# Moving the left tiles by 32 bytes, norm_mix out of the turned blocks, and two pages exchanged, in a hybrid encoder layer

## The chip, the cores and the metric

The kernel runs on one core of one Trainium2 chip. The metric is the device time of one execution in microseconds; lower is better. A core has TensorE (PE; its weight loads are listed apart as PEld), VectorE (DVE), ScalarE (ACT), GpSimd (POOL) and SyncE (SP), which issues most DMAs. Each engine works through its own queue in order.

## The reference, cut to what matters

One layer of an encoder trunk, in float32, on x of 2048 tokens by 1024 features:

```python
h = rms_norm(x, norm_mix[l])
z = h @ w_in[l]
q_a, k_a, v_a, q_b, k_b, v_b, g_a, g_b = jnp.split(z, offsets, axis=-1)
y_a = windowed_gqa(...)       # 8 heads, |t - s| <= 128
y_b = neighborhood_attn(...)  # 8 heads on the 32 x 64 grid of tokens
merged = gates[..., :D] * (y_a @ w_proj_a[l]) + gates[..., D:] * (y_b @ w_proj_b[l])
x = x + merged @ w_out[l]
h2 = rms_norm(x, norm_mlp[l])
x = x + jnp.square(jax.nn.relu(h2 @ w_up[l])) @ w_down[l]
return rms_norm(x, norm_final)
```

rms_norm divides a token's row by its root mean square and multiplies by a gain for each feature.

## The kernel before

**Arithmetic.** Every float32 product is made of three matmuls on float32r parts. An operand t is split into hi (a cast on ACT) and lo (t - hi, on DVE or POOL: `split`, L281), and a product is hi.hi + hi.lo + lo.hi (`mm3`, L199; `mm3s`, L285). In a call `mm3(ps, lh, ll, rh, rl)` the l operands are the weights that TensorE holds (128 x 128) and the r operands are read past them (128 x 512). In a row of the profile such as `zb<-zh,zwhl` zh is read and zwhl is held. The large products for the first 1024 tokens of the input projection, for the up and the down projection are done in two by two blocks with seven block products in place of eight (Strassen's form); the loops over them go through the numbers 1 to 7 in the order 1, 2, 5, 6, 7, 4, 3 (`ORDER`, L352) or another, and each number has its page of right operands, a hi and a lo tile of 128 x 2048 elements: `zh1` to `zh7` in the input projection, `ubh1` to `ubh7` (rows `ubh`) in the up projection.

**Stages, in order of time.** The microseconds are from the span's start, read off the rows.
- 0 to some 380 us: input projection of token blocks 0 and 1 (512 tokens each). x's rows are loaded, normalised, turned by TensorE (`turned`, L274) and multiplied by norm_mix as they leave PSUM (L497 to L501). Nine groups of columns (`QUADS`, L503) are then computed by `in_quad` (L457). Before the last page sums are made, t1 = hi + lo of page 1 is formed on POOL (L537 to L539), placed behind two of the roots that `rstd_of` (L220) computes on POOL.
- Within it, at quads 5 and 6 (L626 to L632), the rows of token blocks 2 and 3 are loaded (`x_tiles`, L343), normalised by DVE (`normalised`, L233) and turned by DVE in blocks of 32 x 32 (`turned_out`, L241), multiplied by norm_mix there (L254, with `gt` from `turned_gain`, L259) and stored to DRAM as h1d.
- 380 to some 1080 us: `h_pages` (L651) loads h1d and splits it into the pages hT, and TensorE alternates between the dense products of blocks 2 and 3 (`mm<-hT,whl`, L200 to L202) and the two attentions.
- 1080 to some 1455 us: gates and output projections (`gated`, L1279), the product with w_out (`pt<-wo,mh`), the residual, and the second norm; `turned_out` writes the turned rows h2d, again with a gain (norm_mlp). For the last of the four token blocks it works in the tile mh (L1339).
- some 1455 to 2080 us: up projection, `up_quad` (L1198), with its pages made by `up_right` (L1131). 2080 us to the end: down projection (L1388 to L1525).

**A turned block's tokens.** Tile t of a block has 128 tokens. A turn in 32 x 32 blocks puts token 128 t + 32 a + c of the block into column 128 a + 32 t + c. Whoever reads h1d or h2d restores the order with `by_place` and `by_token` (L266 to L272).

**Memory.** Each partition of on-chip memory is filled from both ends. Left tiles go upward from 0: 1024 bytes of DMA scratch, four constants at 32 bytes, then the pool cp with ident (512 bytes), g_mix (32), bg (64), sink_t (32), warm and four st tiles (each padded to 32). That makes 1952 bytes, which is 416 modulo 512, and since the tiles behind are whole multiples of 512, all of them lie at 416: zh1, zh2, zh6, zh7, zh4, hT, wo, mh, ml, xr, and the left tiles of the attentions. Right tiles go downward; `power` takes the uppermost 64 bytes, and the others lie at 448 modulo 512: zh5, zh3, zwhl, whl, page, and everything of the up and down projections, whose lowest tile, ubh4, starts at 1984.

Space is used again: a tile that lies where an older one lay waits until that one's last reader is done. In the up projection the homes are given out downward in the order of `up_homes` (L1348), into the place of the output projection's left tiles. Those are, upward: wo to 67488, five xr buffers to 87968, gt to 90016, mh to 106400 and ml to 122784. Page 6 lies at 106432 to 122816, page 2 at 90048 to 106432, and page 3 at 73664 to 90048.

**Order.** The framework orders the instructions of each engine by a simulated timeline when the program is compiled, so they don't run strictly in the order of the source; `tc.issue_after(i)` puts what it encloses behind i on the same engine.

Of the kernel before, what the change touches and what calls it, by code (L numbers as in the profile page):

```python
# [8 lines left out]
F32 = mybir.dt.float32  # L9
F32R = mybir.dt.float32r  # L10
AF = mybir.ActivationFunctionType
ALU = mybir.AluOpType
# [3 lines left out]
D = 1024  # L16
# [6 lines left out]
P = 128  # L23
KC = D // P
NB = 4
BT = 512
# [66 lines left out]
def encoder_layer(ctx, tc, x, norm_mix, w_in, b_gate, sink, rpb, w_pa, w_pb, w_out,  # L93
                  norm_mlp, w_up, w_down, norm_final, dist_a, mask_b, out):
    nc = tc.nc
    V, A, G, PE, SY = nc.vector, nc.scalar, nc.gpsimd, nc.tensor, nc.sync
# [9 lines left out]
    def pools(stack, side, tags, name):  # L106

        return {t: pool(f"{name}_{t}", side=side, stack=stack) for t in tags}

    cp = pool("cp", side="left")  # L110
# [13 lines left out]
    def T(pl, shape, dt, tag, bufs):  # L124
        n_t[0] += 1
        pl = pl[tag] if isinstance(pl, dict) else pl
        return pl.tile(shape, dt, tag=tag, bufs=bufs, name=f"{tag}_{n_t[0]}")
# [2 lines left out]
    ident = cp.tile([P, P], F32, name="ident")  # L130
    make_identity(nc, ident)
    g_mix = cp.tile([P, KC], F32, name="g_mix")
    bg = cp.tile([P, 16], F32, name="bg")
    sink_t = cp.tile([P, AH], F32, name="sink_t")
    power = cr.tile([P, 1], F32, name="power")
    G.memset(power, -0.5)
# [20 lines left out]
    h1d = [dp.tile([D, BT], F32, name=f"h1d{b}") for b in range(2)]  # L157
# [53 lines left out]
    last_dma = [None]  # L211
# [3 lines left out]
        last_dma[0] = SY.dma_start(t, rows).ins  # L215
        return t

    roots = []

    def rstd_of(pl, t, jp=None, mean=False):  # L220

        st = T(pl, [P, 4], F32, "st", 4)
        junk = T(pl if jp is None else jp, [P, 512], F32, "junk", 1)
        for n in range(2):
            A.activation(junk, t[:, n * 512 : (n + 1) * 512], AF.Square, scale=float(D) ** -0.5 if mean else 1.0,
                         accum_out=st[:, n : n + 1])
        r = st[:, 2 : 3]
        V.scalar_tensor_tensor(out=r, in0=st[:, 0:1], scalar=EPS if mean else D * EPS, in1=st[:, 1:2],
                               op0=ALU.add, op1=ALU.add)
        roots.append(G.tensor_tensor(out=r, in0=r, in1=power, op=ALU.pow).ins)  # L230
        return r

    def normalised(pl, tiles, jp=None, by_scalar=False):  # L233

        for t in tiles:
            if by_scalar:
                A.activation(t, t, AF.Copy, scale=rstd_of(pl, t, jp, True))
            else:
                V.tensor_scalar(t, t, rstd_of(pl, t, jp), float(D) ** 0.5, ALU.mult, ALU.mult)

    def turned_out(d, ht, tiles, g, gain=None, queue=None):  # L241

        hv = ht.rearrange("p (j t c) -> p t j c", j=8, t=4)
        for t in range(4):
            V.transpose(out=hv[:, t], in_=tiles[t][:, g * 256 : (g + 1) * 256].rearrange("p (j c) -> p j c", j=8))
        h3 = ht.rearrange("p (j x) -> p j x", j=8)  # L250
        if gain is not None:
            (step, n), _ = gain.ap
            gv = bass.AP(gain.tensor, gain.offset + 8 * g, [[step, n], [1, 8], [0, P]])
            V.tensor_tensor(out=h3, in0=h3, in1=gv, op=ALU.mult)  # L254
        dv = d.rearrange("(j i) (a x) -> a i j x", i=32, a=4)
        for a in range(4):
            (queue or SY).dma_start(dv[a][:, 8 * g : 8 * g + 8], h3[32 * a : 32 * a + 32])

    def turned_gain(t, norm):  # L259

        for a in range(4):
            SY.dma_start(t[32 * a : 32 * a + 32, 32:64], norm[0].rearrange("(j i) -> j i", i=32))
        V.transpose(out=t[:, 0:32], in_=t[:, 32:64])
        return t[:, 0:32]

    def by_token(c):  # L266

        return c.rearrange("p (t a c) -> p t a c", t=4, a=4)

    def by_place(c):  # L270

        return c.rearrange("p (a t c) -> p t a c", t=4, a=4)  # L272
# [5 lines left out]
    def add(eng, out, a, b, op=ALU.add):  # L278
        return eng.tensor_tensor(out=out, in0=a, in1=b, op=op).ins  # L279

    def split(src, hi, lo, eng):  # L281
        A.copy(hi, src)  # L282
        return eng.tensor_tensor(out=lo, in0=src, in1=hi.bitcast(F32), op=ALU.subtract).ins  # L283
# [6 lines left out]
    def halves(t):  # L290

        return t[:, 0:2], t[:, 2:4]
# [13 lines left out]
    xf = x[0]  # L306
    s_z = ExitStack()
# [14 lines left out]
    xp = pools(s_x, "left", ("xin",), "x0")  # L322
# [4 lines left out]
    in_e = ring(s_z, "ze", [P, 2, BT], F32, 2)  # L327
# [15 lines left out]
    def x_tiles(pl, b, bufs):  # L343
        out = []
        for t in range(4):
            xt = T(pl, [P, D], F32, "xin", bufs) if t < bufs else in_v2[0]()
            r = b * BT + t * P
            last_dma[0] = SY.dma_start(xt, xf[r : r + P]).ins
            out.append(xt)
        return out  # L350

# [5 lines left out]

    def left_parts(src, w, eng):
        hl = in_whl()[:, :, :, 0:w]
        split(src, hl[:, 0], hl[:, 1], eng)  # L360
        return hl

    def in_left(ws, w, skip=()):

# [151 lines left out]
    tiles[1] = x_tiles(xp, 1, 8)  # L516
    ws1.append(row_half(*QUADS[1], 1))
    with tc.issue_after(last_dma[0]), nc.allow_non_contiguous_dma(reason="small per-feature vectors"):
        SY.dma_start(bg, b_gate[0].rearrange("(k p) -> p k", p=P))
        SY.dma_start(sink_t, bcast(sink[0], AH))  # L520
    normalised(xp, tiles[0])
    right = {n: (in_page[n](), in_page[n]()) for n in (1, 2)}
    tbanks = [(tpool, 2), (zpool[0], 1), (tpool, 2), (zpool[1], 1), (ypool[0], 1), (ypool[1], 1)]
    for k in range(KC):
        ps = zbank(*tbanks[k % 6])
        turned(ps, tiles[0], k)
        h, l = (t[:, k % 4] for t in right[1 + k // 4])
        scaled(h, ps, k)
        scaled_less(l, ps, k, h.bitcast(F32))
    t1, t3 = in_raw(), in_raw()  # L530
# [3 lines left out]
    next(quad0)  # L534
    next(quad0)
    normalised(xp, tiles[1], by_scalar=True)
    for n, (o, h, l) in enumerate(zip(halves(t1), *map(halves, right[1]))):  # L537
        with tc.issue_after(roots[6 + n]):
            add(G, o, h.bitcast(F32), l.bitcast(F32))  # L539
    next(quad1)  # L540
    next(quad1)

# [7 lines left out]
    for p in range(2):  # L550
        t = T(xp, [P, D], F32, "xin", 8).rearrange("p (k c) -> p k c", k=4)
        c = QUADS[2][0]
        SY.dma_start(t, w_in[0][p * BT : (p + 1) * BT, c : c + 256].rearrange("(k p) f -> p k f", p=P))
        ops2.append(left_parts(t, 256, V))
        next(quad2)
    for n in (5, 3, 6):
        right[n] = (in_page[n](), in_page[n]())
# [5 lines left out]
    for k in range(KC):  # L563
# [8 lines left out]
        else:  # L572
            h, l = (t[:, kk] for t in right[3])
# [41 lines left out]
    for q in range(2, len(QUADS)):  # L615
        if q == 5:
            s_v.close()
            in_v2.pop()
            xp = pools(s_z, "right", ("xin", "st", "gt"), "x2")
            gain = turned_gain(T(xp, [P, 64], F32, "gt", 1), norm_mix)  # L620
        if q == 7:
            bias_tables()
        lf = list(in_left(ws, 256, (1, 2) if q == 2 else ()))
        if q + 1 < len(QUADS):
            ws = in_weights(*QUADS[q + 1])
        if q in (5, 6):  # L626

            b = q - 3
            xt = x_tiles(xp, b, 3)
            normalised(xp, xt, Junk())  # L630
            for g in range(4):
                turned_out(h1d[b - 2], in_e().rearrange("p k x -> p (k x)"), xt, g, gain)  # L632
        ops2.extend(lf if q == 2 else ())
        for _ in quad2 if q == 2 else in_quad(*QUADS[q], iter(lf), right):
            pass
# [15 lines left out]
    def h_pages(b):  # L651
        hi, lo = [], []
        for p in range(2):
            h, l = (T(hpl[2 * (b - 2) + p], PAGE, F32R, "hT", 2) for _ in range(2))
            for n, (hh, ll) in enumerate(zip(halves(h), halves(l))):
                raw = T(wp, [P, KC, P], F32, "raw", 3).rearrange("p (k a) c -> p k (a c)", k=2)
                r = p * BT + n * 256
                SY.dma_start(raw, h1d[b - 2][r : r + 256, :].rearrange("(k p) t -> p k t", p=P))
                for k in range(2):
                    split(by_place(raw[:, k]), by_token(hh[:, k]), by_token(ll[:, k]), V)  # L660
            hi.append(h)
            lo.append(l)
        hp[b] = hi, lo
# [339 lines left out]
    h2d = [dp.tile([D, BT], F32, name=f"h2d{b}") for b in range(NB)]  # L1003
    s_wo = ExitStack()
    pwo = pool("pwo", side="left", stack=s_wo)
    p4x = pools(s_wo, "left", ("xr", "gt", "mh", "ml"), "m")

    p4x["st"] = cp
    gain = turned_gain(T(p4x, [P, BT], F32, "gt", 1)[:, 0:64], norm_mlp)
# [36 lines left out]
    def up_homes(*tags):  # L1046
        made = {}
        for t in tags:
            shape, dt, bufs = {"raw": (PAGE, F32, 5), "whla": ([P, 2, 4, 256], F32R, 1), "whlb": ([P, 2, 4, 256], F32R, 2),
                               "S": ([P, 4, 256], F32, 2), "rb": (PAGE, F32, 1), "chunk": ([P, BT], F32, 4),  # L1050
                               "c": ([P, BT], F32, 11)}.get(t, (PAGE, F32R, 2))
            made[t] = ring(s_up, f"u{t}", shape, dt, bufs)
            if t[:2] == "bh":
                up_page[int(t[2])] = made[t]
        up_rings.update(made)
# [289 lines left out]

    s_pp.close()
    pms.extend(pool(f"pm{i}", space=PSUM) for i in range(8))
    up_homes("bh6", "bh2", "bh3", "chunk", "rb", "c", "bh7", "bh4")  # L1348
    rights, lf = started
    for m in range(2):  # L1350
        right = next(rights)
# [204 lines left out]
```

## Time and profile before

| | |
|---|---|
| time, median of 3 runs | 2700.07 us (2696.72 to 2704.57) |
| the profiled execution | 2699.71 us, span 2697.3 us |
| busy: PE, PEld, DVE, ACT, POOL | 2620.9, 2159.8, 1600.8, 1230.6, 850.4 us |
| mean granted TensorE clock | 0.992 |
| PE busy from 230 to 300 us (input projection, blocks 2 and 3 normalised) | 64.41 of 70.00 us |
| PE busy from 1440 to 1500 us (start of the up projection) | 50.16 of 60.00 us |
| PE busy from 1500 to 2080 us, and from 2080 to 2697 us | 569.69 of 580.00 us, 608.75 of 617.00 us |

The span runs from the first to the last instruction; the execution's time has a little more around it. A row of the groups gives line, engine, operation, tiles, shapes and count, then busy time and mean ns of one, then the engine's idle time just before and what ended it. A row in order of time gives start, duration, the same names, and in brackets the idle time before it. Matmuls overlap in the pipeline, so their durations are longer than the distance from one start to the next; the distance is what a matmul costs.

### The profile page before, as it was taken

The numbers are of one execution on the slowest core, as the hardware profiler recorded it, in microseconds if no ns is written. First come the engines' busy times: TensorE is split into PE (matmuls) and PEld (weight loads), VectorE is DVE, ScalarE is ACT, GpSimd is POOL, SyncE is SP. The second block draws the span as 40 slices with busy tenths as digits, with TensorE's granted clock in tenths as the row PEclk, the third lists the DMA queues.
The fourth block names the chain that finished last, engine by engine and source line by source line (L and its number), as shares of the span: only waits on it lengthen the run. The fifth ranks groups of instructions, "written<-read, shape, count | busy, mean of one in ns | idle before, by whom it ended". The sixth has DMA issues, their size and how long they took to land. (4 is left out here: it accounts for less than half of the span.)

```text
span 2697.3 us, 34681 instructions
## 1 busy us (share of the span) xinstructions
PE 2620.9 (97%) x12140; PEld 2159.8 (80%) x12140; DVE 1600.8 (59%) x2418; ACT 1230.6 (46%) x2257; POOL 850.4 (32%) x671
## 2 busy tenths in 40 slices
PE   7999999999999999999998999999999999999998
PEld 6787777787888888787786888878887888888887
DVE  7766656666444443655657666775565634545766
ACT  6333236666555555623323544454444332323444
POOL 1111223334555542532430455664553000000001
PEclk9999999999999999999999999999999999999999
DMA  5656375446776664854644665764436834445555
GB/s 176 192 155 195 118 236 148 116 113 177 210 223 191 184 180 142 300 157 145 202 144 143 229 224 202 251 232 153 163 113 226 314 140 170 145 149 171 179 192 168
DMA packets 352751, 490.31 MB, mean 182 GB/s; under 512 B 27561, under 2 KB 187433, under 8 KB 350401
## 3 DMA queue, kind: packets, MB, share of 16 engines
q1 hardware_dynamic: 345664, 471.31, 55.1%
q10 hardware_dynamic: 6912, 16.78, 1.7%
q8 instruction: 96, 1.57, 0.2%
q14 instruction: 79, 0.64, 0.1%
HBM read 328.55 MB, written 159.45 MB: 181 GB/s over the span
## 5 line engine op out<-in xcount | busy, mean ns | idle before, releaser
L287 PE MATMUL b<-dwh,dah 128*128 128x512 f32 x896 | 348.9, 389 | 0.0
L288 PE MATMUL b<-dwh,dah 128*128 128x512 f32 x896 | 348.0, 389 | 0.0
L286 PE MATMUL b<-dwh,dah 128*128 128x512 f32 x896 | 339.3, 391 | 2.0 <-ACT dwh L282 2.0
L279 POOL TENSOR_TENSOR uc<-uc,uc 128x512 f32<-128x512 f32 x120 | 235.8, 1980 | 196.8 <-ACT uc L1196 161.5
L282 ACT CAST dah<-da 128x1024 fp32r<-128x1024 f32 (+1 forms) x128 | 121.0, 945 | 366.2 <-PE b L288 242.7
L283 DVE TENSOR_TENSOR dah<-da,dah 128x1024 fp32r<-128x1024 f32 (+1 forms) x128 | 139.2, 1089 | 221.2 <-ACT dah L282 217.2
L286 PE MATMUL b<-ubh,uwhlb 128*128 128x512 f32 x592 | 230.6, 390 | 4.4 <-DVE uc L279 1.7
L288 PE MATMUL b<-ubh,uwhlb 128*128 128x512 f32 x592 | 229.6, 389 | 1.1 <-DVE uwhlb L283 1.1
L287 PE MATMUL b<-ubh,uwhlb 128*128 128x512 f32 x592 | 230.3, 389 | 0.0
L200 PE MATMUL mm<-hT,whl 128*128 128x512 f32 x544 | 220.2, 405 | 0.0
L201 PE MATMUL mm<-hT,whl 128*128 128x512 f32 x544 | 216.5, 398 | 0.0
L202 PE MATMUL mm<-hT,whl 128*128 128x512 f32 x544 | 216.3, 398 | 0.0
L177 POOL TENSOR_TENSOR whl<-raw,whl 128x1024 fp32r<-128x1024 f32 x66 | 165.6, 2510 | 158.8 <-ACT whl L176 140.4
L1446 POOL TENSOR_TENSOR st<-st,power 128x1 f32<-128x1 f32 x16 | 13.5, 857 | 615.8 <-DVE st L1445 615.8
L286 PE MATMUL zb<-zh,zwhl 128*128 128x512 f32 x476 | 190.8, 402 | 12.1 <-DVE zc L279 6.3
L286 PEld LDWEIGHTS b<-dwh,dah 128*128 128x128 f32 x896 | 168.7, 188 | 37.5 <-ACT dwh L282 2.4
L287 PEld LDWEIGHTS b<-dwh,dah 128*128 128x128 f32 x896 | 168.5, 188 | 35.1
L288 PEld LDWEIGHTS b<-dwh,dah 128*128 128x128 f32 x896 | 168.4, 188 | 35.0
L279 DVE TENSOR_TENSOR uc<-b,uc 128x512 f32<-128x512 f32 x160 | 108.4, 687 | 143.0 <-PE b L288 128.5
L287 PE MATMUL zb<-zh,zwhl 128*128 128x512 f32 x476 | 190.0, 399 | 0.0
L288 PE MATMUL zb<-zh,zwhl 128*128 128x512 f32 x476 | 187.3, 399 | 1.8 <-DVE zwhl L283 1.8
L286 PEld LDWEIGHTS b<-ubh,uwhlb 128*128 128x128 f32 x592 | 111.1, 188 | 28.9 <-issue 2.4
(250 smaller groups left out, 6192.0 us busy)
## 6 DMA issues: line engine op xcount, KB each, us to landing
at<-uc SPq DMA_DIRECT2D x224, 256.0 KB
da<-at SPq DMA_DIRECT2D x96, 512.0 KB
dw<-in_w_down_dram SPq DMA_DIRECT2D x160, 256.0 KB
uraw<-in_w_up_dram SPq DMA_DIRECT2D x32, 1024.0 KB
raw<-in_w_in_dram SPq DMA_DIRECT2D x34, 512.0 KB
zraw<-in_w_in_dram SPq DMA_DIRECT2D x16, 1024.0 KB
z<-zg SPq DMA_DIRECT2D x64, 256.0 KB
qa<-qs_a SPq DMA_DIRECT2D x32, 256.0 KB
```

What stands on the lines that cost most here:

```text
L177: G.tensor_tensor(out=hl[:, 1], in0=raw, in1=hl[:, 0].bitcast(F32), op=ALU.subtract)
L200: PE.matmul(ps, lh, rh, start=first, stop=False)
L201: PE.matmul(ps, lh, rl, start=False, stop=False)
L202: PE.matmul(ps, ll, rh, start=False, stop=last)
L279: return eng.tensor_tensor(out=out, in0=a, in1=b, op=op).ins
L282: A.copy(hi, src)
L283: return eng.tensor_tensor(out=lo, in0=src, in1=hi.bitcast(F32), op=ALU.subtract).ins
L286: PE.matmul(ps, lh, rh, start=first, stop=False, skip_group_check=True)
L287: PE.matmul(ps, lh, rl, start=False, stop=False, skip_group_check=True)
L288: PE.matmul(ps, ll, rh, start=False, stop=last, skip_group_check=True)
L1446: G.tensor_tensor(out=r, in0=r, in1=power, op=ALU.pow)
```

## The change

Six edits. bg is allocated with 24 columns in place of 16, of which 16 are used; the left tiles behind it lie 32 bytes higher, at 448 modulo 512. For token blocks 2 and 3, x's rows are loaded so that tile t holds tokens 128 a + 32 t + c, and the turned columns then stand in the tokens' own order. norm_mix is no longer multiplied into the turned blocks; `h_pages` applies it while it splits, as the scale of ACT's copy and in DVE's subtraction. The normalisation of these two blocks goes from DVE (`tensor_scalar`) to ACT (an activation with a scale). The two adds that make t1 go from POOL to DVE, behind the lo part of the first extra operand of quad 2. And two pairs of homes change places: gt and xr on the left side, and the up projection's pages 2 and 3.

```diff
-    bg = cp.tile([P, 16], F32, name="bg")
+    bg = cp.tile([P, 24], F32, name="bg")
...
-        roots.append(G.tensor_tensor(out=r, in0=r, in1=power, op=ALU.pow).ins)
+        G.tensor_tensor(out=r, in0=r, in1=power, op=ALU.pow)
...
             r = b * BT + t * P
-            last_dma[0] = SY.dma_start(xt, xf[r : r + P]).ins
+            rows = xf[r : r + P]
+            if b > 1:
+
+                rows = bass.AP(xf.tensor, xf.offset + (b * BT + t * 32) * D, [[P * D, 4], [D, 32], [1, D]])
+            last_dma[0] = SY.dma_start(xt, rows).ins
...
-        split(src, hl[:, 0], hl[:, 1], eng)
+        last_part[0] = split(src, hl[:, 0], hl[:, 1], eng)
...
-        SY.dma_start(bg, b_gate[0].rearrange("(k p) -> p k", p=P))
+        SY.dma_start(bg[:, 0:16], b_gate[0].rearrange("(k p) -> p k", p=P))
...
-    for n, (o, h, l) in enumerate(zip(halves(t1), *map(halves, right[1]))):
-        with tc.issue_after(roots[6 + n]):
-            add(G, o, h.bitcast(F32), l.bitcast(F32))
...
         ops2.append(left_parts(t, 256, V))
+        if p == 0:
+            with tc.issue_after(last_part[0]):
+                for o, h, l in zip(halves(t1), *map(halves, right[1])):
+                    add(V, o, h.bitcast(F32), l.bitcast(F32))
...
-            xp = pools(s_z, "right", ("xin", "st", "gt"), "x2")
-            gain = turned_gain(T(xp, [P, 64], F32, "gt", 1), norm_mix)
+            xp = pools(s_z, "right", ("xin", "st"), "x2")
...
-            normalised(xp, xt, Junk())
+            normalised(xp, xt, Junk(), by_scalar=True)
             for g in range(4):
-                turned_out(h1d[b - 2], in_e().rearrange("p k x -> p (k x)"), xt, g, gain)
+                turned_out(h1d[b - 2], in_e().rearrange("p k x -> p (k x)"), xt, g)
...
                 for k in range(2):
-                    split(by_place(raw[:, k]), by_token(hh[:, k]), by_token(ll[:, k]), V)
+                    gain = g_mix[:, p * 4 + n * 2 + k : p * 4 + n * 2 + k + 1]
+                    A.activation(hh[:, k], raw[:, k], AF.Copy, scale=gain)
+                    V.scalar_tensor_tensor(out=ll[:, k], in0=raw[:, k], scalar=gain, in1=hh[:, k].bitcast(F32),
+                                           op0=ALU.mult, op1=ALU.subtract)
...
-    p4x = pools(s_wo, "left", ("xr", "gt", "mh", "ml"), "m")
+    p4x = pools(s_wo, "left", ("gt", "xr", "mh", "ml"), "m")
...
-    up_homes("bh6", "bh2", "bh3", "chunk", "rb", "c", "bh7", "bh4")
+    up_homes("bh6", "bh3", "bh2", "chunk", "rb", "c", "bh7", "bh4")
```

More of the change, by code (lines that the diff above doesn't have):

```diff
@@ L216, in load_tile @@
         return t
-    roots = []
     def rstd_of(pl, t, jp=None, mean=False):
@@ L359, in left_parts @@
         hl = in_whl()[:, :, :, 0:w]
-        split(src, hl[:, 0], hl[:, 1], eng)
+        last_part[0] = split(src, hl[:, 0], hl[:, 1], eng)
         return hl
+    last_part = [None]
     def in_left(ws, w, skip=()):
```

## The prediction

> **What bounds the kernel now.** I read the page's busy table first, then the groups of instructions, then TensorE's rows in order of time, then its waits.
>
> ```profile
> PE 2620.9 (97%) x12140; PEld 2159.8 (80%) x12140; DVE 1600.8 (59%) x2418; ACT 1230.6 (46%) x2257; POOL 850.4 (32%) x671
> ...
> L287 PE MATMUL b<-dwh,dah 128*128 128x512 f32 x896 | 348.9, 389 | 0.0
> ...
> L201 PE MATMUL mm<-hT,whl 128*128 128x512 f32 x544 | 216.5, 398 | 0.0
> ...
> L287 PE MATMUL zb<-zh,zwhl 128*128 128x512 f32 x476 | 190.0, 399 | 0.0
> ...
> L201 PE MATMUL pt<-wo,mh 128*128 128x512 f32 x256 | 99.9, 392 | 0.0
> ```
>
> TensorE is busy for 97% of the span and no other engine for more than 59%. So time goes only in two ways: a matmul that takes longer than it must, or a gap on TensorE. The four groups have one shape. In the first and the last both operands lie on one side of the memory (dwh and dah right, wo and mh left): 389 and 392 ns. In the two between, which read left pages against right weights (zb's right pages among them), it is 398 and 399 ns. Left tiles start at 416 modulo 512 bytes, right ones at 448.
>
> Means hold stalls, so I compare bare runs. In the fourth quad products 3 and 4 take turns, twelve matmuls each; 3 reads the right page zh3, 4 the left page zh4, both against zwhl on the right. The last two rows are from the down projection, 24 matmuls apart.
>
> ```profile
> 161.36 0.39 PE L286 MATMUL zb<-zh,zwhl 128*128 128x512 f32 x1
> ...
> 164.11 0.40 PE L286 MATMUL zb<-zh,zwhl 128*128 128x512 f32 x1
> ...
> 166.91 0.39 PE L286 MATMUL zb<-zh,zwhl 128*128 128x512 f32 x1
> ...
> 169.65 0.40 PE L286 MATMUL zb<-zh,zwhl 128*128 128x512 f32 x1
> ...
> 2299.63 0.39 PE L286 MATMUL b<-dwh,dah 128*128 128x512 f32 x1
> ...
> 2305.07 0.39 PE L286 MATMUL b<-dwh,dah 128*128 128x512 f32 x1
> ```
>
> Start to start, the right page takes 2.75/12 = 229 ns (first run) and 2.74/12 = 228 ns (third), the left page between them 2.80/12 = 233 ns, the down projection 5.44/24 = 227 ns. Same stage, same weights, same microseconds: the difference goes with the page's place.
>
> The second loss is a gap, the longest once the first rows are in.
>
> ```profile
> PE b L286 <- ACT ubh L282: 8.2, 1, 8.2
> ...
> 1466.47 0.39 PE L287 MATMUL b<-ubh,uwhlb 128*128 128x512 f32 x1
> 1475.09 1.22 PE L286 MATMUL b<-ubh,uwhla 128*128 128x512 f32 x2 [8.22 <-ACT ubh L282]
> ...
> 1480.78 0.47 PE L288 MATMUL b<-ubh,uwhla 128*128 128x512 f32 x1
> ...
> 1475.00:1481.00 6.00, 5.87 (x13) 4.19 (x14) 5.93 (x6) 4.05 (x6) 0.00 (x0) 0.51 0.01 3
> ...
> 1464.57 1.04 ACT L282 CAST uwhlb<-uraw 128x1024 fp32r<-128x1024 f32 x1 [5.08 <-PE b L288]
> 1473.99 1.99 ACT L282 CAST ubh<-urb 128x1024 fp32r<-128x1024 f32 x2 [8.38 <-DMA h2d<-mh]
> ...
> 1463.08 8.50 SPq L257 DMA_DIRECT2D h2d<-mh  x16
> ...
> 1459.21 1.41 DVE L249 STREAM_TRANSPOSE mh<-xr 128x256 f32<-128x256 f32 x4
> 1460.55 5.91 DVE L254 TENSOR_TENSOR mh<-mh,gt 128x1024 f32<-128x1024 f32 x4
> 1475.07 2.36 DVE L283 TENSOR_TENSOR ubh<-urb,ubh 128x1024 fp32r<-128x1024 f32 x2 [8.61 <-ACT ubh L282]
> ```
>
> TensorE waits 8.2 us for the first cast of page 2 of the up projection. ACT could not write it before 1473.99, because the page lies on mh, from which the last block's h2 is still being stored: 16 issues, 8.50 us of SP's queue. Afterwards the granted clock is 0.51: from 1475.09 to 1480.78 twelve matmuls take 5.69 us, against 12 x 0.227 = 2.72, another 3.0 us.
>
> **The change, part by part.**
>
> Left tiles 32 bytes higher. bg grows from 64 to 96 bytes, so every left tile after it moves from 416 to 448 modulo 512, where the right ones lie. It concerns the matmuls of a left page against right weights: hT with whl, 3 x 544 = 1632, and of zb's 3 x 476 = 1428 the five products of seven whose pages are left (1, 2, 6, 7, 4), 1020; together 2652. wo with mh stays a pair on one side. Each saves at least 233.3 - 228.7 = 4.6 ns (zh4 against its neighbours), 12.2 us; at most 233.3 - 226.7 = 6.6 ns (down projection), 17.5 us. I take 14: the neighbours of a page will be aligned too, but these stages have more traffic beside them than the down projection. The trace has no pair moved by 32 bytes and all else alike, so a saving of nothing stays open and is a rival. There is a rule against this part: the Trainium skill (TensorE: Matmul & The Clock Gate, "Step-by-step: what each phase is for") says that PE has two independent SBUF read ports and that loading the next weights takes nothing from the running matmul. By that rule the relative place of page and weights could not matter, and this term would be 0; the 228 to 229 against 233 ns above disagree with it.
>
> Pages 2 and 3 change places. Page 3 now lies on mh, page 2 on four of the five xr buffers; gt, which was in page 3's region, goes below xr and out of both. What page 2 then waits for is the last transpose out of xr, at 1459.21 + 1.41 = 1460.62; its source urb was issued long before, at 1441.63:
>
> ```profile
> 1441.63 0.36 SPq L1136 DMA_DIRECT2D urb<-h2d  x1
> ```
>
> ACT is free at 1464.57 + 1.04 = 1465.61, so the cast ends at 1466.65, where TensorE now begins to wait. The second matmul needs the low part from DVE, which multiplies by gt until 1460.55 + 5.91 = 1466.46; with half of the 2.36 us behind it, that is 1467.7. The wait of 8.2 us shrinks to about 1; the 3.0 us at half clock go with it: 10.2. Late next is DVE, which has two subtractions for page 7 to make between the splits; I leave 0.2 for that and take 10. Page 3, the last product, waits for mh's stores instead; these end at 1473.99, and three products of 24 matmuls stand before it (3 x 24 x 0.227 = 16.3 us from 1466.7, so 1483). At most 12 is saved (DVE splits before it multiplies), at least 4 (ACT takes page 3's cast too early and is blocked by those stores).
>
> norm_mix moves out of the turned blocks. These rows stand for the input projection's late quads.
>
> ```profile
> L254 DVE TENSOR_TENSOR ze<-ze,gt 128x1024 f32<-128x1024 f32 x8 | 11.2, 1420 | 0.0
> ...
> L239 DVE TENSOR_SCALAR xin<-xin,st 128x1024 f32<-128x1024 f32 x6 | 4.4, 730 | 1.5 <-POOL st L230 1.4
> L239 DVE TENSOR_SCALAR zv<-zv,st 128x1024 f32<-128x1024 f32 x2 | 2.4, 1178 | 0.0
> ...
> L282 ACT CAST zwhl<-zraw 128x1024 fp32r<-128x1024 f32 x9 | 9.4, 1044 | 25.4 <-PE zb L288 25.4
> ...
> L237 ACT ACTIVATE xin<-xin,st x4: 1137/1146/1150, 24.1 to 34.0; 128x1024 f32<-128x1024 f32 x4
> ...
> 254.03 0.50 PE L286 MATMUL zb<-zh,zwhl 128*128 128x512 f32 x1 [1.19 <-ACT zwhl L282]
> ...
> 257.48 0.79 PE L286 MATMUL zb<-zh,zwhl 128*128 128x512 f32 x1 [2.71 <-DVE zc L279]
> ...
> 262.97 0.40 PE L286 MATMUL zb<-zh,zwhl 128*128 128x512 f32 x1
> ...
> 234.68 2.67 POOL L230 TENSOR_TENSOR st<-st,power 128x1 f32<-128x1 f32 x3
> 236.92 2.65 POOL L283 TENSOR_TENSOR zwhl<-zraw,zwhl 128x1024 fp32r<-128x1024 f32 x1
> ```
>
> DVE loses eight multiplies (11.2 us) and eight normalisations (4.4 + 2.4), 18.0 us in all; ACT gains eight at 1.146 us, 9.2 us, in a stage in which it sits idle 25.4 us for TensorE before the weight casts alone. TensorE's waits on this path are 1.19 + 2.71 us, and the 13 matmuls from 257.48 to 262.97 take 5.49 us where 13 x 0.229 is 2.98: 2.5 more. All gone would be 6.4. But an ACT that scales must first wait for POOL's root, and the weight casts stand behind it in the same queue: one root behind a POOL split (2.65) with the scaling (1.15) costs 3.8. So the bounds are -6.4 and +3.8; I take -3, the half of what can go.
>
> The rest I put at 0. In the pages of h, 16 casts become scaled copies and 16 subtractions become scaled ones:
>
> ```profile
> L282 ACT CAST hT<-raw x16: 615/620/624, 349.9 to 377.3; 128x512 fp32r<-128x512 f32 x16
> L283 DVE TENSOR_TENSOR hT<-raw,hT x16: 679/686/2860, 350.5 to 378.3; 128x512 fp32r<-128x512 f32 x16
> ...
> L498 ACT ACTIVATE zh<-zb,g_mix x12: 678/708/765, 13.5 to 46.2; 128x512 fp32r<-128x512 f32 x12
> ...
> L424 DVE SCALAR_TENSOR_TENSOR z<-mm,z x10: 678/686/692, 393.8 to 515.6; 128x512 fp32r<-128x512 f32 x10
> ```
>
> That is 16 x 0.09 = 1.4 us more on ACT, behind TensorE's work on the last quads, and nothing on DVE. x's eight loads keep their number, 128 rows of 4 KB each, in another order. At the start two adds leave POOL for DVE:
>
> ```profile
> 32.36 1.21 DVE L283 TENSOR_TENSOR zwhl<-xin,zwhl 128x1024 fp32r<-128x1024 f32 x1
> 38.97 1.22 DVE L283 TENSOR_TENSOR zwhl<-xin,zwhl 128x1024 fp32r<-128x1024 f32 x1 [5.40 <-ACT zwhl L282]
> ...
> L254 DVE TENSOR_TENSOR ht<-ht,gt x12: 1179/1756/3420, 1183.6 to 1378.9; 128x1024 f32<-128x1024 f32 x12
> ```
>
> They are ordered behind the first of these splits, and DVE then sits idle 5.40 us; an add of this shape costs it what the split costs, so 2.4 us lie inside the gap. Without that cover it would be 2.4 on the path. The four small gt loads leave SP's queue here. The other gt's loads wait for an older buffer, some microseconds later, and the first multiply by it is only at 1183.6 (last row). Sum: -14 - 10 - 3 = -27. The profiled execution took 2699.7 us (2697.3 of span, 2.4 around it), so 2672.7; the median shown is 0.4 above it: **2673**.
>
> **Rivals.** (a) The place of a page costs nothing, and the 4.6 ns come from something else that left pages share: only 10 + 3 are left, 2687. For it: no 32-byte move is in the trace; against it, wo lies at the very addresses of hT, left, and takes 392 ns with left weights. (b) The wait at page 2 is handed on, to DVE's low parts or to page 3's cast blocking ACT: of 10 only the half clock or less remains, 0 to 3, and with 14 + 3 - or 14 alone - the time is 2680 to 2686, say 2683. For it: DVE has no idle time in the six microseconds after 1475 (5.93 of 6.00 busy). Against: those are splits that now start 7 us earlier. (c) Slower: ACT, now waiting for roots, becomes the bound of the late quads. Each of eight scalings would wait behind a POOL split and the roots before it, 2.65 + 2.67 = 5.3 us, 42.6 in all, with weight casts queued behind: 2699.7 - 24 + 42.6 = 2718. It decides from 8 x 4.4 us on, where the 27 and 8 more are used up. Against it: ACT's 25.4 idle us, and nothing on TensorE needs these rows until the quads are done. (d) The instruction order shifts with the new costs and the gaps only move: about 2697.
>
> **How the numbers follow.** Forecast 0.66, (a) 0.10, (b) 0.14, (c) 0.05, (d) 0.05. The terms' bounds give 2699.7 - 17.5 - 12 - 6.4 = 2664 at the low end; I go to 2661 for gaps that vanish unasked. Upward, 14, 4 and +3.8 give 2685, (a) and (b) lie at 2683 to 2687; (a) with the second term at its low bound would be 2693, and I stop at 2691. A change under 0.3% (8 us) can't be told from none: (c) is slower, (d) is the same and so is a little of (a), the rest is faster: 0.88, 0.07, 0.05.
>
> **What would show it.** In the changed profile the zb and mm groups should have means of 389 to 393 ns, and a left page's twelve matmuls should take 2.72 to 2.75 us; 2.80 proves the first term wrong. The wait of TensorE for ubh should be under 2 us, with a clock near 1.00 behind it, and ACT's wait for mh's stores should be gone or stand before page 3. The late quads should show no multiply by gt, DVE some 18 us lighter, and the waits at 254 and 257 shorter; a new wait of ACT for POOL's root above 2 us, several times, would be rival (c). The prediction fails if the first term is under 8 us or the second under 4.

## The result and the profile after

| | median | runs | ratio to before, 95% interval |
|---|---|---|---|
| before | 2700.34 us | 16 | 1 |
| changed | 2706.73 us | 16 | 1.0021 [1.0014, 1.0029] |

2673 us was predicted, with a range from 2661 to 2691. The changed kernel takes 2706.7: it lost 6 us, where 27 were to be gained. It is slower beyond doubt, though by less than the 0.3% that was named as the bound of no change.

The groups of the changed kernel's page that answer to those shown of before (busy time, mean ns of one, idle time of TensorE before them and what ended it):

```profile
PE 2609.1 (96%) x12140; PEld 2161.5 (80%) x12140; DVE 1589.7 (59%) x2403; ACT 1238.9 (46%) x2265; POOL 846.0 (31%) x669
...
L284 PE MATMUL zb<-zh,zwhl 128*128 128x512 f32 x476 | 191.2, 403 | 29.0 <-DVE zc L277 15.3 <-ACT zwhl L280 6.6 <-ACT ze L452 4.4
...
L201 PE MATMUL mm<-hT,whl 128*128 128x512 f32 x544 | 214.1, 394 | 0.0
```

TensorE is busy 11.8 us less than before, and yet the span is 7.0 us longer (2704.3 against 2697.3): the work shrank and the gaps grew. The means show only half of it. mm fell from 398 to 394 ns, while zb stayed at 398 to 403: behind its gaps, 29.0 us of them in the row above, TensorE runs at half clock for a while, and 57 of zb's 1428 matmuls take over 500 ns where 25 did before. So, as before, bare runs in TensorE's order of time, from the fourth quad; rows twelve matmuls apart:

```profile
162.44 0.39 PE L284 MATMUL zb<-zh,zwhl 128*128 128x512 f32 x1
...
165.16 0.39 PE L284 MATMUL zb<-zh,zwhl 128*128 128x512 f32 x1
...
167.88 0.39 PE L284 MATMUL zb<-zh,zwhl 128*128 128x512 f32 x1
```

2.72 us and 2.72 us, 227 ns a matmul, whichever of pages 3 and 4 is read. Before it was 2.75 and 2.80. In the up projection the wait for ubh is 0.7 us instead of 8.2, at full clock (TensorE's waits there as total, times and longest in us, and the stretch behind, with the granted clock third from the right):

```profile
PE b L285 <- DVE ubh L281: 0.7, 1, 0.7
```

```profile
1478.00:1490.00 12.00, 10.56 (x45) 7.92 (x43) 12.00 (x10) 5.63 (x6) 1.22 (x1) 1.00 0.74 182
```

Both large steps of the prediction are there. Where the time went is seen by stage, from the first matmul on hT, on page, on ubh and on dwh in each trace:

| | start to hT | hT to page | page to ubh | ubh to dwh | dwh to end |
|---|---|---|---|---|---|
| before | 380.3 | 696.0 | 349.2 | 652.1 | 619.7 |
| changed | 396.8 | 696.7 | 349.3 | 643.3 | 618.1 |

The up projection gives 8.8 us. The input projection, which should have become shorter, takes 16.5 more. Its late quads, in stretches with the busy time (and count) of PE, PEld, DVE, ACT and POOL, the granted clock, the share of the 16 DMA engines and GB/s, and TensorE's four gaps there:

```profile
230.00:242.00 12.00, 5.43 (x18) 4.14 (x17) 1.52 (x4) 5.05 (x12) 3.47 (x3) 0.72 0.30 102
242.00:262.00 20.00, 14.14 (x61) 11.07 (x61) 13.59 (x29) 8.37 (x13) 3.50 (x3) 0.98 0.66 190
262.00:275.00 13.00, 13.00 (x46) 10.40 (x47) 6.69 (x6) 4.08 (x7) 0.00 (x0) 0.77 0.49 172
275.00:292.00 17.00, 11.71 (x52) 9.38 (x50) 1.37 (x5) 6.70 (x17) 1.65 (x3) 0.99 0.19 78
292.00:300.00 8.00, 3.36 (x8) 2.71 (x9) 4.78 (x10) 4.91 (x6) 4.45 (x3) 0.50 0.44 124
```

```profile
237.60 0.77 PE L284 MATMUL zb<-zh,zwhl 128*128 128x512 f32 x1 [6.57 <-ACT zwhl L280]
246.18 0.47 PE L284 MATMUL zb<-zh,zwhl 128*128 128x512 f32 x1 [1.43 <-DVE zc L277]
261.76 0.80 PE L284 MATMUL zb<-zh,zwhl 128*128 128x512 f32 x1 [4.42 <-ACT ze L452]
296.64 0.76 PE L284 MATMUL zb<-zh,zwhl 128*128 128x512 f32 x1 [9.93 <-DVE zc L277]
```

In these 70 us TensorE works 47.65, where it was 64.41 before. The releasers named are DVE and ACT, but neither is busy: between 275 and 292 DVE works 1.37 of 17 us. They are late because of something else. The longest gap, followed back through the engines' orders of time (the last row is TensorE's from above):

```profile
266.57 3.33 SPq L350 DMA_DIRECT2D zv<-in_x_dram  x1
...
289.02 0.63 ACT L223 ACTIVATE ze<-zv 128x512 f32<-128x512 f32 x1 [3.28 <-DMA zv<-in_x_dram]
...
290.39 0.16 DVE L226 SCALAR_TENSOR_TENSOR st<-st 128x1 f32<-128x1 f32 x1 [9.30 <-ACT ze L223]
292.22 1.63 DVE L247 STREAM_TRANSPOSE ze<-xin 128x256 f32<-128x256 f32 x4
294.01 1.22 DVE L281 TENSOR_TENSOR zwhl<-zraw,zwhl 128x1024 fp32r<-128x1024 f32 x1 [0.16 <-ACT zwhl L280]
...
295.84 1.25 DVE L277 TENSOR_TENSOR zc<-zb,zc 128x512 f32<-128x512 f32 x2
```

Read from the bottom: the addition that empties a PSUM tile stands on DVE behind transposes of x's rows and a weight split; these stand behind the sum of squares that DVE has waited 9.30 us for; ACT forms these squares, and right ahead of them, in its own order, come some of the last tile's, for whose load it had waited 3.28 us. That load was issued at 266.57 and ACT could begin on it at 289.02, over 22 us later. The loads are slow, and in a queue that works in order everything behind their first reader is late with them. In the changed kernel's list of ACT's waits for this stage they add up:

```profile
ACT ze L223 <- DMA xin<-in_x_dram: 16.1, 5, 5.3
...
ACT ze L223 <- DMA zv<-in_x_dram: 3.3, 1, 3.3
```

Why they are slow shows in the DMA view of the same kernel from 268 to 288 us, where nearly nothing but the second block's loads is moved (packets, MB, share of 16 engines):

```profile
DMA packets 500, 2.00 MB, mean 100 GB/s; under 512 B 15, under 2 KB 15, under 8 KB 499
...
q1 hardware_dynamic: 499, 1.98, 25.1%
```

25.1% of 16 engines is as much as four engines that are constantly busy, at 100 GB/s together. Before, the second block's 2 MB came between 253 and 261 us, with stores beside them; two stretches of that time:

```profile
254.00:257.00 3.00, 0.73 (x2) 0.30 (x2) 3.00 (x4) 0.00 (x0) 0.00 (x0) 0.76 0.97 365
257.00:260.00 3.00, 2.52 (x5) 1.66 (x6) 3.00 (x4) 0.00 (x0) 0.00 (x0) 0.50 1.00 311
```

There all engines work, at 311 to 365 GB/s. The new load names its rows as 4 runs of 32 rows of 1024 elements, so its outermost dimension is 4, and the old one's was 128. The Trainium skill (DMA: Bandwidth & Descriptors, "Why a DMA increments its semaphore by 16 and not by 1") says that such a DMA uses the largest number of engines up to 16 that divides the slowest dimension of both its patterns; for 4 and 128 that is 4, and the 25.1% agree.

### The profile page after: what moved, and what is told of

It reads as the page before. It is cut to its first block, busy times and chain, and to the rows that moved or that the text cites. A ratio compares the mean times of both kernels' runs of the same rounds, so it can differ in the third digit from the quotient of the medians.

```text
span 2704.3 us, 34675 instructions
## 1 busy us (share of the span) xinstructions
PE 2609.1 (96%) x12140; PEld 2161.5 (80%) x12140; DVE 1589.7 (59%) x2403; ACT 1238.9 (46%) x2265; POOL 846.0 (31%) x669
## 5 line engine op out<-in xcount | busy, mean ns | idle before, releaser
L284 PEld LDWEIGHTS zb<-zh,zwhl 128*128 128x128 f32 x476 | 92.1, 194 | 52.5 <-ACT zwhl L280 12.1
```

What stands on the lines that cost most here:

```text
L284: PE.matmul(ps, lh, rh, start=first, stop=False, skip_group_check=True)
```

## The experiments

The theory: A, the place of the left tiles, and B, the pages' exchange, bring what was predicted; C, norm_mix's move, brings little; and the loads on four engines cost all of it and more. The main rival: ACT's new work and the order without roots make the loss, and the loads' order is free.

Kernels that are compared ran beside the kernel before on one chip: the first four together, then four, then two; before's median was 2701.54, 2701.27 and 2701.87 us. Ratios are to before, and a gain in us is worked out from the ratio and that median; it differs by up to 3 us from the difference of the two medians. With the loads alone, and with C and plain rows (e10, e4, e7), the tokens of blocks 2 and 3 stand in another order; these kernels leave out what would restore it and are read for their times alone.

| run | what it has | median, us | ratio, 95% interval |
|---|---|---|---|
| `e1_left_up` | A | 2686.29 | 0.9938 [0.9926, 0.9950] |
| `e3_homes_alone` | B | 2699.93 | 0.9988 [0.9979, 0.9996] |
| `e8_place_and_homes` | A, B | 2681.25 | 0.9928 [0.9909, 0.9947] |
| `e10_norm_alone` | C | 2700.36 | 0.9990 [0.9981, 0.9999] |
| `e2_loads_alone` | the loads | 2721.49 | 1.0070 [1.0057, 1.0082] |
| `e4_plain_rows` | A, B, C | 2679.49 | 0.9912 [0.9897, 0.9928] |
| `e5_four_loads` | A, B, C, loads in four | 2681.59 | 0.9928 [0.9909, 0.9947] |
| `e6_two_engines` | A, B, C, loads in two | 2747.33 | 1.0169 [1.0147, 1.0191] |
| `e7_plain_rows_dve` | A, B, most of C | 2682.62 | 0.9929 [0.9909, 0.9949] |
| `e9_four_loads_qa4` | as e5, one buffer more | 2695.54 | 0.9966 [0.9952, 0.9979] |

And their traces by stage, as above. Each line is one execution, and executions of one kernel spread over some 10 us (before from 2696.30 to 2706.83 in the first batch), so that a difference of a microsecond or two in a stage says little:

| | start to hT | hT to page | ubh to dwh |
|---|---|---|---|
| before | 380.3 | 696.0 | 652.1 |
| A | 376.5 | 693.3 | 648.0 |
| B | 379.9 | 699.7 | 650.6 |
| A, B | 377.8 | 691.0 | 644.0 |
| C | 373.1 | 703.8 | 655.3 |
| the loads | 404.1 | 699.6 | 650.9 |
| A, B, C | 371.2 | 697.2 | 643.5 |
| A, B, C, loads in four | 368.4 | 698.8 | 644.3 |
| the changed kernel | 396.8 | 696.7 | 643.3 |

### The left tiles alone

```diff
-    bg = cp.tile([P, 16], F32, name="bg")
+    bg = cp.tile([P, 24], F32, name="bg")
-        SY.dma_start(bg, b_gate[0].rearrange("(k p) -> p k", p=P))
+        SY.dma_start(bg[:, 0:16], b_gate[0].rearrange("(k p) -> p k", p=P))
```

> The kernel before with the left tiles at 448 modulo 512 and nothing else. Theory: 233.3 ns a 128x512 matmul of the products 1, 2, 6, 7, 4 and 232 ns of the first up projection's come down to 227, as in the changed kernel's trace, and little of it is eaten by waits: 2686 to 2690 us, the zb groups without half-clock stretches at 390 to 395 ns and dwh's first matmul 10 to 14 us earlier. Rival: the matmuls shorten but the pages that they wait for come no earlier, as the first up projection of the changed kernel kept its 696 us: 2694 to 2700 us, with a longer wait of TensorE for DMA qa<-qs_a and the q pages.

Measured: 2686.3 us. A ratio of 0.9938 is 16.7 us of 2701.5 (13.5 to 20.0). Groups of this kernel:

```profile
L201 PE MATMUL mm<-hT,whl 128*128 128x512 f32 x544 | 214.9, 395 | 0.0
...
L287 PE MATMUL zb<-zh,zwhl 128*128 128x512 f32 x476 | 188.1, 395 | 0.0
```

398 and 399 ns became 395, by 32 bytes and nothing else. Start to start over all undisturbed matmuls of a page, a left page of the input projection falls from 233.3 to 227.2 ns and hT from 232.8 to 229.1; even the right page zh3 falls from 228.7 to 227.2, so part of what it took lay with its neighbours. By count that is 1020 x 6.1 = 6.2 us in the input projection and 1632 x 3.7 = 6.0 in hT's stage (which the expectation calls the first up projection), 12.2 in all. The stages show 3.8 and 2.7 of it; TensorE's wait for the qa page, behind hT's start, has grown from 2.9 to 5.8 us. The two profiled executions differ by 10.4 us of span, somewhat less than the timed ones. Another 4.1 us come from the up projection, whose steps stand in another order here: the 8.2-us wait for ubh has become one of 3.3 us for uwhlb. ACT's order shows what moved:

```profile
1459.12 1.99 ACT L282 CAST ubh<-uraw 128x1024 fp32r<-128x1024 f32 x2
1468.96 2.00 ACT L282 CAST ubh<-urb 128x1024 fp32r<-128x1024 f32 x2 [7.84 <-DMA h2d<-mh]
```

Page 2, from urb, still waits for mh's stores. The page from uraw is page 3, and it is cast ahead of page 2, where before it came behind it, at 1475.89. In the kernel before page 3 ends at 90048 and mh begins at 90016, so that it lay on 32 bytes of mh as well; the move takes it off. That this order is why TensorE waits less is argued from the addresses and these rows; no run tries it by itself. So the rival, that the pages eat what the matmuls save, is right for a part of hT's stage and wrong for the whole. By the rule of two independent read ports (the Trainium skill, TensorE: Matmul & The Clock Gate, "Step-by-step: what each phase is for"), which the prediction weighed, this run should have shown nothing; its 395 against 398 and 399 ns disagree.

### The pages' places alone, and with the left tiles

```diff
-    p4x = pools(s_wo, "left", ("xr", "gt", "mh", "ml"), "m")
+    p4x = pools(s_wo, "left", ("gt", "xr", "mh", "ml"), "m")
-    up_homes("bh6", "bh2", "bh3", "chunk", "rb", "c", "bh7", "bh4")
+    up_homes("bh6", "bh3", "bh2", "chunk", "rb", "c", "bh7", "bh4")
```

> The kernel before with the two exchanges of pages' places (gt with xr, bh2 with bh3) and nothing else. Theory: the wait of 8.2 us for ubh at 1475 us and the 3.0 us of half clock behind it are gone, nothing takes their place: 2689 to 2693 us. Rival: the wait is handed on to a later page: 2697 to 2701 us, with a new wait of TensorE of 4 us or more between 1450 and 2100 us.

Measured: 2699.9 us, 3.2 of 2701.5 us gained (1.1 to 5.7). The theory fails. The time is the rival's, and the wait was handed on, but to the same page and not to a later one. TensorE's waits, and in order of time the engines' rows at page 2:

```profile
PE b L287 <- DVE ubh L283: 8.0, 1, 8.0
```

```profile
1466.29 8.75 SPq L257 DMA_DIRECT2D h2d<-mh  x16
...
1468.76 1.99 ACT L282 CAST ubh<-urb 128x1024 fp32r<-128x1024 f32 x2
...
1477.26 2.36 DVE L283 TENSOR_TENSOR ubh<-urb,ubh 128x1024 fp32r<-128x1024 f32 x2 [7.59 <-DMA h2d<-mh]
```

The cast no longer waits for mh's stores, but now the low part does, on the other engine. That is what rival (b) of the prediction had named. The addresses tell why: page 2 now reaches from 73664 to 90048, its low part being the upper half, and mh, still at 416, begins at 90016. They share 32 bytes, enough for the whole wait. The left tiles' move puts mh at 90048, and it fits. That makes a forecast for the two edits together:

> The kernel before with the left tiles at 448 and both exchanges of pages' places, and nothing else. The exchange alone left an 8.0-us wait, now of VectorE's low part: page 2 then reaches from 73664 to 90048 and mh begins at 90016. Theory (those 32 bytes are what it waits for, and the move by 32 bytes takes them away): no wait above 2 us for ubh, and the two parts together are worth more than their sum of 16.7 and 3.2 us: 2674 to 2680 us. Rival (the wait follows from the order of SP's stores whatever the bytes): 2681 to 2688 us, with a wait of 4 us or more for ubh.

The whole of TensorE's list of waits from 1440 to 1530 us with both:

```profile
PE b L288 <- POOL uwhlb L283: 1.7, 1, 1.7
PE b L286 <- DVE uc L279: 1.6, 2, 1.2
PE b L286 <- ACT uwhlb L282: 0.7, 1, 0.7
PE b L287 <- DVE ubh L283: 0.7, 1, 0.7
PE b L288 <- POOL uwhla L283: 0.2, 1, 0.2
```

The wait is gone, and the low part is now made while mh's stores are still being issued, so it no longer waits for them:

```profile
1454.87 8.59 SPq L257 DMA_DIRECT2D h2d<-mh  x16
...
1458.17 2.35 DVE L283 TENSOR_TENSOR ubh<-urb,ubh 128x1024 fp32r<-128x1024 f32 x2
```

The up projection takes 644.0 us, 8.0 less than before, where A alone gives 4.1 and B alone 1.5. The time, 2681.25 us, missed the theory's 2674 to 2680 and lies in the rival's range, though without the rival's wait: the two are worth 19.4 us (14.3 to 24.6), and their separate gains add up to 19.9. That they are worth more together than apart is seen only in this stage of the trace, not in the time.

### norm_mix alone

In the kernel before: by_scalar in `normalised`, `turned_out` without a gain, the gain in `h_pages`, t1's sum on VectorE, as in the diff of the change; the rest as before.

> The kernel before with norm_mix taken out of the turned blocks and into the page's parts, the multiplication by the root on ScalarE, and t1 added on VectorE; left tiles at 416, pages' places and x's loads as before, so that the tokens of blocks 2 and 3 stand in another order. Theory (my predicted third term, 3 us with bounds of a gain of 6.4 and a loss of 3.8): 2694 to 2704 us, no TensorE gap above 4 us between 230 and 300 us. Rival (this part loses by itself some of what the changed kernel lost): 2706 us or more, with waits for zwhl or ze as in the changed kernel.

Measured: 2700.4 us, a gain of 2.7 (0.3 to 5.1), within what was predicted. TensorE's waits from 215 to 445 us:

```profile
PE s L737 <- DMA qa<-qs_a: 10.8, 1, 10.8
PE zb L284 <- DVE zc L277: 3.6, 2, 3.0
PE zb L284 <- ACT ze L448: 2.9, 1, 2.9
```

No wait for zwhl and none above 4 us in the quads: ACT carries the scaling without trouble, and the rival falls. The stages tell more than the sum. The input projection is 7.2 us shorter, more than twice what was predicted for it, and hT's stage is 7.8 us longer: TensorE comes to the first attention earlier and there waits for its page qa, 10.8 us instead of 2.9. The up projection is 3.2 us longer as well. This one execution's span is 2.1 us above before's (2699.4 against 2697.3), so the stages show where time went and not the gain of 2.7.

### The loads alone

```diff
-            last_dma[0] = SY.dma_start(xt, xf[r : r + P]).ins
+            rows = xf[r : r + P]
+            if b > 1:
+                rows = bass.AP(xf.tensor, xf.offset + (b * BT + t * 32) * D, [[P * D, 4], [D, 32], [1, D]])
+            last_dma[0] = SY.dma_start(xt, rows).ins
```

> The kernel before with the eight loads of x's blocks 2 and 3 taken in four runs of 32 rows (4, 32 and 1024 elements as dimensions) and nothing else; the rows of the two blocks enter in another order. Theory: the load is served by four DMA engines because its outermost dimension is 4; each of its 512 KB takes about 5.6 us instead of 2, ScalarE's squares wait for DMA xin about 7 us longer in all, and TensorE waits for ze, zc and zwhl behind them, some of it at half clock: 2716 to 2730 us, the two blocks' packets spread over some 22 us at about 80 GB/s. Rival: the loss of the changed kernel comes from norm_mix's multiplication on ScalarE and from the removed order behind the roots, and the loads' order is without a price, as I had predicted: 2698 to 2703 us, packets over 8 us.

Measured: 2721.5 us, 18.9 lost (15.4 to 22.2). This is the step that the prediction put at 0. The queue's share from 264 to 270 us, before stores come in beside, and TensorE's two long gaps:

```profile
q1 hardware_dynamic: 138, 0.55, 24.8%
```

```profile
245.61 0.77 PE L286 MATMUL zb<-zh,zwhl 128*128 128x512 f32 x1 [10.08 <-DVE zc L279]
...
287.61 0.80 PE L286 MATMUL zb<-zh,zwhl 128*128 128x512 f32 x1 [12.69 <-ACT ze L452]
```

A quarter of the engines here too, and the input projection takes 23.8 us longer.

### The changed kernel with plain rows

> The changed kernel with x's rows of blocks 2 and 3 loaded as before, 128 rows in a row for each tile, and nothing else; the tokens of the two blocks therefore stand in another order. Theory (four DMA engines): the packets of the second block's loads lie within 8 us again, TensorE's gaps of 6.6, 4.4 and 9.9 us between 230 and 300 us shrink below 2 us, and the predicted sum comes through: 2672 to 2682 us. Rival (norm_mix on ScalarE, additions of t1 on VectorE or roots no longer ordered are the loss): the gaps stay, 2698 to 2707 us. Half and half would give about 2690 us.

Measured: 2679.5 us; the input projection takes 371.2 us, 25.6 less than in the changed kernel, and the gaps of 6.57 and 9.93 us are gone. TensorE's waits from 215 us to hT's first matmul:

```profile
PE zb L284 <- DVE zc L277: 5.3, 2, 3.3
PE zb L284 <- ACT ze L448: 2.1, 1, 2.1
```

With plain rows the change gains 23.8 us (19.5 to 27.8), where all its parts were predicted to gain 27. The rivals fall.

### How many engines

If it is the number of engines and not the rows' order, the same rows must come quickly with another outermost dimension, and more slowly with 2:

```diff
 # four loads of 32 rows
+                for a in range(4):
+                    last_dma[0] = SY.dma_start(xt[32 * a : 32 * a + 32], xf[b * BT + a * P + t * 32 : b * BT + a * P + t * 32 + 32]).ins
 # two loads of 2 x 32 rows
+                for a in range(2):
+                    rows = bass.AP(xf.tensor, xf.offset + (b * BT + 2 * a * P + t * 32) * D, [[P * D, 2], [D, 32], [1, D]])
+                    last_dma[0] = SY.dma_start(xt[64 * a : 64 * a + 64], rows).ins
```

> The changed kernel with each x tile of blocks 2 and 3 loaded by four loads of 32 rows, to the same partitions as in the changed kernel; the outermost dimension of a load is then 32 instead of 4, and SP issues 24 loads more, at some 0.4 us each. Theory (a load whose outermost dimension is 4 goes through four engines, one of 32 through all): packets of the second block within 8 to 12 us, TensorE's gaps behind ze and zc as short as with plain rows, 2676 to 2684 us. Rival: not the number of engines but the order in memory (rows of 4 KB, 2 MB apart) makes the load slow, or the queue is held up by the 24 further issues: 2700 us and more.

> The changed kernel with each x tile of blocks 2 and 3 loaded by two loads of 64 rows whose outermost dimension is 2, to the same partitions. Theory: each load goes through two engines, and if both loads of a tile share the same two, the four tiles of a block take some 45 us instead of 22 and ScalarE waits for them about 20 us longer than in the changed kernel: 2725 to 2760 us, DMA share over the loads 0.12 or less. Rival (the loads' rate has another cause than the outermost dimension): within 5 us of the changed kernel, 2702 to 2712 us, at a rate of 78 GB/s as there.

The queue's row while the second block is loaded, with four loads from 250 to 262 us, with two from 300 to 325:

```profile
q1 hardware_dynamic: 1093, 2.67, 88.3%
```

```profile
DMA packets 328, 1.30 MB, mean 52 GB/s; under 512 B 10, under 2 KB 10, under 8 KB 328
...
q1 hardware_dynamic: 328, 1.30, 12.8%
```

The four runs of a tile lie 512 KB apart (128 rows of 4 KB), not 2 MB as the first expectation has it, and the changed kernel and these two read the same ones. The same rows in the same places: 32 outermost keeps all engines at work, 4 gives 25.1% and 100 GB/s, 2 gives 12.8%, two engines, and 52 GB/s. By the Trainium skill's rule quoted above (DMA: Bandwidth & Descriptors, "Why a DMA increments its semaphore by 16 and not by 1") it should be 16, 4 and 2 engines; the three shares agree. The times follow: 2681.6, 2706.7 and 2747.3 us. Nor is it the number of loads under way: two loads for a tile are slower than one. Four loads keep the right order of tokens and gain 19.4 us on before (14.3 to 24.6); the 24 further issues of SP (twelve of a block's sixteen take 6.45 and 6.33 us of its queue) cost nothing that shows. This kernel and the one with A and B alone are the fastest that leave the tokens in their order, and they can't be told apart: with its loads put right, norm_mix's move adds nothing that shows.

### The root's multiplication back on VectorE

```diff
-            normalised(xp, xt, Junk(), by_scalar=True)
+            normalised(xp, xt, Junk())
```

> The changed kernel with plain rows (as in the run with plain rows, 2679.5 us) and the multiplication by the root of blocks 2 and 3 back on VectorE; the tokens of the two blocks stand in another order. Theory (my predicted term for norm_mix, about 3 us, with ScalarE and VectorE trading some 8 us each): within 4 us of 2679.5. Rival 1 (ScalarE's multiplication behind the root holds up the casts, part of what the changed kernel loses): 2670 to 2675 us. Rival 2 (VectorE is what the late quads lack): 2683 to 2690 us.

Measured: 2682.6 us, 3.1 above the run with plain rows, with intervals that overlap. Which of the two engines multiplies makes no difference that shows. The time lies within the theory's 4 us and 0.4 below rival 2's range; a cost of 2 or 3 us on VectorE can't be excluded.

### A fourth buffer for qa

```diff
-        q = T(ap_, [P, 4, P], F32R, "qa", 3)
+        q = T(ap_, [P, 4, P], F32R, "qa", 4)
```

> The changed kernel with four loads of 32 rows for each x tile of blocks 2 and 3 (2681.6 us) and, beside that, four buffers instead of three for the page qa of the first attention. In that kernel TensorE waits 9.0 us at 405 us for DMA qa<-qs_a, against 2.9 us in the kernel before; it is where a part of what the shorter matmuls save goes. Theory (the load is issued late, at 409 us, because all three buffers are still being read): the wait falls below 4 us, 2672 to 2678 us. Rival (the issue is late for another reason, SP's queue or the order of the attention's own steps, or the wait goes to the next page): 2679 to 2685 us, a wait of 5 us or more there.

Measured: 2695.5 us, slower than both had it. TensorE's waits from 390 to 470 us and from 685 to 730:

```profile
PE s L741 <- DMA qa<-qs_a: 0.7, 1, 0.7
...
PE s L902 <- DMA kb<-ks_b: 7.6, 2, 4.7
PE s L902 <- DMA qb<-qs_b: 7.3, 1, 7.3
```

The buffer does what the theory says of it, 0.7 instead of 9.0 us, but hT's stage takes 712.9 us instead of 698.8: 14.9 us of waits for kb and qb stand in front of the second attention, where it is 2.5 us with three buffers, and from 690 to 740 us the granted clock is 0.80 in place of 1.00. Why its loads come so late wasn't tried.

## Why the prediction was wrong

**The failed step** is a sentence among what was put at 0: "x's eight loads keep their number, 128 rows of 4 KB each, in another order." Number, rows and bytes are indeed the same. What changed is the shape of the list, and with it the engines that serve a load. Alone it costs 18.9 us; in the changed kernel 2706.7 stands against 2679.5 with plain rows, 27 us. No term, rival or bound of the prediction contained it, so that even a range of 30 us missed, and of the two signs of failure that it named, the first term under 8 us or the second under 4, neither came. The question that its own method asks, what waits for the moved transfer and which work hides it, would have led to it. ACT waited for these loads before the change already, so that nothing covered them (its waits from 210 to 345 us in that trace):

```profile
ACT ze L225 <- DMA xin<-in_x_dram: 8.5, 2, 7.1
```

**Place of the left tiles, -14.** Right in mechanism: the matmuls became shorter. By count that is 12.2 us, the low bound; hT gained 3.7 ns a matmul, less than the lower bound of 4.6. That the whole came to 16.7 is partly luck: the stages show only 6.5 us where these matmuls stand, and 4.1 came from the order of the up projection, which isn't in this term. Rival (a) falls.

**Pages 2 and 3, -10.** Right in the changed kernel (8.8 us by the stage, the wait at 0.7 us, the clock at 1.00). As an edit by itself it is worth 3.2, as in rival (b): the prediction treated it as a step of its own and didn't see that it needs the 32 bytes of the step before it.

**norm_mix, -3.** 2.7 measured (0.3 to 5.1), but not as half of what can go: in the trace 7.2 us are gained in its stage and 7.8 lost in the next, so that the agreement is luck.

**The sum.** Without the loads 2679.5 was reached, against 2673. What is missing is in hT's stage, which takes 697.2 us instead of 696.0, though its matmuls became 6.0 us shorter and two parts let it begin 9.1 us earlier: the qa page is waited for 8.8 instead of 2.9 us. This is rival (d) in one place, gaps that move. That the wait by itself is the cause isn't shown, since the run that took it away with a fourth buffer was slower. The prediction's upward sum takes 14 for the first term where its low bound is 12.2; with that it is 2687 in place of 2685, still inside its range.

**Rival (c), 2718,** came near in time and named the engine that is late, but not its cause: it has ACT waiting for POOL's roots, and the changed kernel's ACT waits 19.4 us for loads of x; no wait of ACT for a root stands among its waits in this stage. Its argument against itself, ACT's 25.4 idle us, was of no use, since an engine in front of a late load is idle as well.

**What was to show it.** The twelve matmuls at 2.72 us, the ubh wait and the clock came out. The means of 389 to 393 ns did not: 398 to 403 for zb, in which matmuls at half clock are counted, and 394 to 401 for mm, whose distance fell to 229 ns and not to 227. Why hT's matmuls stay above the others is open.

## What to carry to other kernels

When a load's pattern is rewritten, look at its outermost dimension, not only at its bytes and rows: a load of 4 runs of 32 rows kept a quarter of the engines busy, and four loads of 32 rows nearly all. When a tile is moved to end a wait, compare first and last byte with what lies there: 32 shared bytes kept all of the 8 us. And a gain in one stage counts only if the next stage's loads come earlier too: here 7.2 us won in front of an attention stand against 7.9 us more of waiting for its page.

## What the runs showed of the hardware

In the input projection a 128x512 matmul on float32r parts takes 233.3 ns from start to start when the page read starts at 416 modulo 512 and the weights at 448, and 227.2 when both start at 448; 32 bytes of an unrelated tile decide it. In the kernel before, wo with mh, both at 416, takes 227.5, so it is the difference of the two places that costs, not the place 416. Why is open, and only this one pair of places was tried. A load with 4 outermost took 25.1% of the 16 engines and moved 100 GB/s, one with 2 12.8% and 52 GB/s: some 25 GB/s for an engine, at packets of 4 KB, an estimate that counts these shares as four and two engines.
